# Narrow gate weights in a tile of their own, loaded behind five x tiles, with an x ring of five slots

## The chip, the core and the metric

The kernel runs on one core of a Trainium2 chip. The metric is the device time of one execution in microseconds. Before the change three timed runs took 2071.55, 2075.75 and 2076.64 us; their median, 2075.75, is the time that the change is measured against.

## The reference, cut to what matters

One decoder layer works on x of 1024 tokens by 2048 features. Its first step is an RMS norm and one wide projection; the last 16 of the 8208 columns are the narrow gates, b and a, of the delta-rule heads.

```
h = rms_norm(x, norm_w)
proj = einsum('btd,dc->btc', h, w_in)            # w_in: 2048 x 8208
q1, q2, k1, k2, v_da, gate_da = ...              # columns 0 to 4095, differential attention
qkv, z = ...                                     # columns 4096 to 8191, gated DeltaNet
b_raw = proj[..., 8192:8200]                     # narrow gates
a_raw = proj[..., 8200:8208]
...
return x + einsum('btc,cd->btd', mixed, w_out)   # then the final RMS norm
```

## The kernel before

The wide projection is done as two-level block products: the tokens are split into two halves and the features into two halves, and seven products of sums of blocks (the list ORDER) replace eight plain ones. The left operands are the weights, 256 columns per job, the right operands are seven combinations of the normalised and transposed x: B11, B21 and B22 are blocks, T1 to T4 differences of blocks. Each is kept in SBUF as a high and a low float16 part ("h" and "l", the tiles hb).

The start of the kernel makes these operands. Eight tiles of 128 tokens are taken in the order SEQ = 4, 0, 5, 1, 6, 2, 7, 3, that is in four pairs, one tile of each token half. For each tile, `scales` has ScalarE square both halves and sum them (jkw<-xt) and GpSimd take the power (rs); `scale` has VectorE multiply each half by rs and the norm weights (xt<-xt,rs,nwb). Then `combine` takes over: `turn` transposes four 128x128 blocks at a time on TensorE into PSUM banks (bka, bkb, side), `sums` and `make` subtract T1, T3, T2 and T4 on VectorE (the profile calls these tiles T), and `parts` splits everything into high and low parts, on ScalarE, VectorE or GpSimd. T1 to T4 have one buffer each. A tile of x is free once its last block is transposed ("turned").

The narrow weights, 2048 rows of 16 columns, are loaded once (abw). `narrow` squares and sums them on ScalarE, finds a scale over TensorE, VectorE and GpSimd, and writes the scaled high part on ScalarE and the low part on VectorE (abst). `narrow_sums` multiplies them with the finished token columns in four steps. Before the change abw lies in the buffer of T4 (line 791), so the first T4 waits for "abst" (lines 697 and 698).

The weights of the wide jobs are loaded as raw tiles (`weights`, `room`), two per job, three buffers. For each job ScalarE squares four blocks (jkw<-raw), TensorE, VectorE and GpSimd find the scales (f, sc), and seven products' weights are split into whi (ScalarE) and wlo (VectorE). The first two products of the first job, `early`, run column by column while the start goes on; all others (`products`) run at full width afterwards.

All loads of the start go through one SyncE queue. What is issued when, on it and on the engines, is decided when the program is built: `Planner` keeps one lane per task, books each instruction and each transfer with a cost (Op.cost, `transfer`), and always emits the instruction that could start first by this book. The engines then follow that order, each instruction waiting for its operands. `transfer` (lines 203 to 214) books pieces of up to 1024 bytes from w_in with 0.15 us each, sixteen at a time; a transfer's data count as there 2 us after its end (LAND).

Of the kernel before, what the change touches and what calls it, by code (L numbers as in the profile page):

```python
# [11 lines left out]
F32 = mybir.dt.float32  # L12
# [11 lines left out]
D = 2048  # L24
H = 8
P = 128
NT = T // P
ND = D // P
# [15 lines left out]
def bcast_rows(ap, n=P):  # L44
    return bass.AP(tensor=ap.tensor, offset=ap.offset, ap=[[0, n], *ap.ap])
# [220 lines left out]
class Planner:  # L266
# [104 lines left out]
    def dma(self, out, in_, bulk=False):  # L371
        self.pending.append(Copy(out, in_, bulk))
        self.nw[out.name] = self.nw.get(out.name, 0) + 1
        self.nr[in_.name] = self.nr.get(in_.name, 0) + 1
# [93 lines left out]
def hybrid_trunk(ctx: ExitStack, tc: tile.TileContext, a, out):  # L468
# [4 lines left out]
    dma = plan.dma  # L473
# [21 lines left out]
    w_v = w_in.rearrange("(a p) c -> p a c", p=P)  # L495
# [23 lines left out]
    done = set()  # L519
    box = {}  # L520

    def when(*keys):
        return lambda: all(k in done for k in keys)

    def junk(n):
        return cst.tile([P, D // 2], BF16, "jkw")[:, :n]
# [34 lines left out]
    def wide():  # L561
        return ps.tile([P, 512], F32, "prod", 2)
# [11 lines left out]
    def pow2_floor(dst, src):  # L574
        yield pool.tensor_tensor(out=dst, in0=src, in1=mhalf[:, :free_len(dst)], op=ALU.pow)
        yield dve.tensor_scalar(out=dst.bitcast(I32), in0=dst.bitcast(I32), scalar1=0x7F800000, scalar2=None,
                                op0=ALU.bitwise_and)
# [4 lines left out]
    SEQ = (4, 0, 5, 1, 6, 2, 7, 3)  # L582
    xt = {}

    def normalise(xs, abw):
        nwb = xs.tile([P, D], F32, "nwb")
        nw16 = xs.tile([P, ND], F32, "nw16")
        dma(nw16, a["norm_w"][0].rearrange("(p a) -> p a", p=P))
        half_d = [slice(k * (D // 2), (k + 1) * (D // 2)) for k in range(2)]

        def load(m):
            if m >= 4:
                yield when(("turned", m - 4))
            t = xt[SEQ[m]] = xs.tile([P, D], F32, "xt", 4)
            dma(t, x[SEQ[m] * P:(SEQ[m] + 1) * P, :])
            done.add(("loaded", m))

        def rest():
            for m in range(4, 8):
                yield from load(m)  # L600
        for m in range(2):
            yield from load(m)
        for sl in half_d:
            dma(nwb[:, sl], bcast_rows(a["norm_w"][0, sl]))
        dma(abw, w_v[:, :, 8192:8208])
        for m in range(2, 4):
            yield from load(m)
        done.add("loads")
        s_rest.push(rest())
        dma(gdn_w, a["gdn_norm_w"].rearrange("o p -> p o"))  # L610
        dma(sub_w, a["da_subln_w"].rearrange("o p -> p o"))
        nmx = xs.tile([P, 2], F32, "nmx")
        yield dve.tensor_reduce(out=nmx[:, 0:1], in_=nw16, axis=AX.X, op=ALU.max)
        yield dve.tensor_reduce(out=nmx[:, 1:2], in_=nw16, axis=AX.X, op=ALU.min, negate=True)
        yield dve.tensor_tensor(out=nmx[:, 0:1], in0=nmx[:, 0:1], in1=nmx[:, 1:2], op=ALU.max)
        pt = wide()
        yield pe.transpose(out=pt[:1, :P], in_=nmx[:, 0:1], identity=ident)
        big = xs.tile([1, 1], F32, "big")
        yield dve.tensor_reduce(out=big, in_=pt[:1, :P], axis=AX.X, op=ALU.max)
        yield dve.tensor_scalar(out=big, in0=big, scalar1=1e-18, scalar2=2.0 ** -7, op0=ALU.max, op1=ALU.mult)  # L620
        yield dve.tensor_tensor(out=big, in0=big, in1=big, op=ALU.mult)
        yield pe.matmul(pt[:, :1], ones[:1], big, start=True, stop=True)
        hsq = xs.tile([P, 1], F32, "hsq")
        yield dve.tensor_copy(hsq, pt[:, :1])
        hsc = xs.tile([P, 1], F32, "hsc")
        yield from pow2_floor(hsc, hsq)
        yield dve.reciprocal(hun, hsc)
        rs = {}

        def scales():  # L630
            for m, tb in enumerate(SEQ):
                yield when(("loaded", m))
                ss = xs.tile([P, 2], F32, "ss", 2)
                for k, sl in enumerate(half_d):
                    yield act.activation(junk(D // 2), xt[tb][:, sl], AF.Square, accum_out=ss[:, k:k + 1])
                ms = xs.tile([P, 1], F32, "ms", 2)
                yield dve.tensor_tensor(out=ms, in0=ss[:, 0:1], in1=ss[:, 1:2], op=ALU.add)
                yield dve.tensor_scalar(out=ms, in0=ms, scalar1=1.0 / D, scalar2=EPS, op0=ALU.mult, op1=ALU.add)
                if m >= 4:
                    yield when(("normed", SEQ[m - 4], 1))  # L640
                r = xs.tile([P, 1], F32, "rs", 4)
                yield pool.tensor_tensor(out=r, in0=ms, in1=mhalf[:, 0:1], op=ALU.pow)
                yield pool.tensor_tensor(out=r, in0=r, in1=hsc, op=ALU.mult)
                rs[tb] = r

        def scale():
            for i in range(4):
                pair = SEQ[2 * i:2 * i + 2]
                for k, sl in enumerate(half_d):
                    for tb in pair:  # L650
                        yield lambda: tb in rs
                        yield dve.scalar_tensor_tensor(out=xt[tb][:, sl], in0=xt[tb][:, sl], scalar=rs[tb],
                                                       in1=nwb[:, sl], op0=ALU.mult, op1=ALU.mult)
                        done.add(("normed", tb, k))

        s_scales.push(scales())
        s_scale.push(scale())

    def combine(xs):
        turns = [(n, nm) for n in range(8) for nm in ("B12", "B11", "B22", "B21")]  # L660
        turned, gone = [0], set()
# [32 lines left out]
        def make(n, m, l, r):  # L694
            if n:
                yield when(("split", m, n - 1))
            elif m == "T4":
                yield when("abst")
            t = sb[m, n] = xs.tile([P, 512], F32, m)
            yield dve.tensor_tensor(out=t, in0=l, in1=r, op=ALU.subtract)  # L700
            done.add((m, n))
# [51 lines left out]
    abu = small("abu", [P, 1])  # L753

    def narrow(xs, abw):
        yield when("loads")
        abst = xs.tile([P, ND, 32], F16, "abst")
        abq = xs.tile([P, 1], F32, "abq")
        f2 = xs.tile([P, 1], F32, "abf")
        abs_ = xs.tile([P, 1], F32, "abs")  # L760
        pt = box["ab"] = ps.tile([P, 512], F32, "av")
        yield act.activation(junk(256).rearrange("p (a c) -> p a c", a=ND), abw, AF.Square, accum_out=abq)
        yield pe.matmul(pt[:, :1], ones, abq, start=True, stop=True)
        yield dve.tensor_scalar(out=f2, in0=pt[:, :1], scalar1=2.0 ** -28, scalar2=1e-37, op0=ALU.mult, op1=ALU.max)
        yield from pow2_floor(abs_, f2)
        yield act.activation(abst[:, :, :16], abw, AF.Copy, scale=abs_)
        yield dve.scalar_tensor_tensor(out=abst[:, :, 16:], in0=abw, scalar=abs_, in1=abst[:, :, :16],
                                       op0=ALU.mult, op1=ALU.subtract)
        done.add("abst")
        yield dve.reciprocal(abu, abs_)  # L770
        s_nsum.push(narrow_sums(abst))

    def narrow_sums(abst):
        pt = box["ab"]
        for i in range(4):
            yield when(("cols", i))
            cs = slice(i * P, (i + 1) * P)
            for m, (n, g, r) in enumerate(NARROW):
                bh, bl = hb[n]
                c0 = (r * 4 + i) * 32  # L780
                for k in range(NH):
                    yield pe.matmul(pt[:, c0:c0 + 32], bh[:, k, cs], abst[:, g * NH + k], start=m < 3 and k == 0,
                                    stop=False, block=i)
                    yield pe.matmul(pt[:, c0:c0 + 16], bl[:, k, cs], abst[:, g * NH + k, :16], start=False,
                                    stop=m != 2 and k == NH - 1, block=i)
        done.add("narrow")

    def startup():
        with ExitStack() as st:
            xs = rpool(st, "xs")  # L790
            abw = xs.tile([P, 512], F32, "T4")[:, :256].rearrange("p (a c) -> p a c", a=ND)
            s_norm.push(normalise(xs, abw))
            s_narrow.push(narrow(xs, abw))
            yield from combine(xs)
            yield when("narrow", ("cols", 3))
        box["ev"] = rpool(right, "ev")
        lead.push(decay())
        lead.push(acc_loads())
# [917 lines left out]
    z_job(6)  # L1716

    outputs.push(startup())
    weights_.push(weights())
    main.push(products())  # L1720
# [207 lines left out]
```

## Time and profile before

| | us |
|---|---|
| profiled execution | 2082.34 |
| its span | 2080.6 |
| PE busy in the span | 1922.2 |
| VectorE busy | 1533.1 |
| ScalarE busy | 1058.7 |
| GpSimd busy | 362.2 |
| median of three timed runs | 2075.75 |

Times are taken from one profiled execution, counted from the start of its span. PE is TensorE, DVE is VectorE, ACT is ScalarE, POOL is GpSimd and SPq is the queue in which SyncE issues transfers. Nearly all instructions have line 369, because the planner emits them there; they are told apart by the tiles that they write and read.

### The profile page before, as it was taken

What the parts mean: (1) busy time and instruction counts of PE and PEld (TensorE: products, weight loads), DVE (VectorE), ACT (ScalarE), POOL (GpSimd) and SP (SyncE); (2) the same over time, 40 slices, a digit from 0 to 9 for tenths busy, and PEclk for the clock granted to TensorE, in tenths of its full rate; (3) what the DMA queues carried; (4) which work ended last, traced back from release to release, by engine and by line L of the source; (5) the groups of instructions that cost most, each with busy time, mean ns of one, the idle gap of its engine ahead of it and who ended that gap; (6) DMA issues with size and microseconds to landing.
All of it is one profiled execution on the core that took longest, in us unless ns stands there. A gap on an engine that the chain in (4) does not pass through costs nothing.

```text
span 2080.6 us, 28925 instructions
## 1 busy us (share of the span) xinstructions
PE 1922.2 (92%) x10221; PEld 1185.3 (57%) x10221; DVE 1533.1 (74%) x2831; ACT 1058.7 (51%) x2261; POOL 362.2 (17%) x383
## 2 busy tenths in 40 slices
PE   3699999999998899998999999899998999999896
PEld 3644455444443345454665555455555888888785
DVE  6776877877999973789887879788897566645343
ACT  6645555554344434476665657565675334434122
POOL 4503113220212201111212111111122110210000
PEclk7699999999999999998999999999999999999998
DMA  9046566456435686643557754555345676737322
GB/s 244 3 94 166 115 152 184 111 155 179 122 61 69 107 167 154 155 114 102 146 143 128 136 107 111 126 116 132 100 119 186 204 229 227 235 139 282 108 89 101
DMA packets 234498, 292.28 MB, mean 140 GB/s; under 512 B 51745, under 2 KB 160497, under 8 KB 231921
## 3 DMA queue, kind: packets, MB, share of 16 engines
q1 hardware_dynamic: 234352, 290.43, 54.6%
q8 instruction: 81, 1.33, 0.3%
q14 instruction: 65, 0.52, 0.1%
HBM read 206.44 MB, written 85.50 MB: 140 GB/s over the span
## 4 chain that ended last, share of the span: by engine, by line
PE 65%; DVE 14%; DMA 10%; issue 4%; ACT 4%; POOL 2%; SPq 1%; POOLq 0%; DVEq 0%; ACTq 0%
PE prod L369 43%; PE bka L369 6%; PE bkb L369 6%; PE av L369 5%; PE side L369 4%; DVE wlo L369 2%; DMA raw<-in_w_in_dram 2%; DVE c L369 2%; DVE raw L369 1%; SPq L401 1%; DVE A L369 1%; ACT jkw L369 1%; DVE tmp L369 1%; ACT whi L369 1%; DMA gq<-c 1%
## 5 line engine op out<-in xcount | busy, mean ns | idle before, releaser
L369 PEld LDWEIGHTS <-whi 128*128 128x128 f16 x3680 | 360.3, 100 | 410.2 <-issue 42.4
L369 PEld LDWEIGHTS <-wlo 128*128 128x128 f16 x1840 | 184.2, 100 | 210.9 <-DVE wlo L369 20.4
L369 ACT ACTIVATE whi<-raw,sc 128x1024 f16<-128x1024 f32 x160 | 182.6, 1146 | 207.7 <-PE prod L369 111.1
L369 DVE SCALAR_TENSOR_TENSOR wlo<-raw,sc,whi 128x1024 f16<-128x1024 f32 x160 | 206.1, 1293 | 20.9 <-ACT whi L369 20.6
L369 ACT ACTIVATE jkw<-raw 128x1024 bf16<-128x1024 f32 x140 | 147.2, 1051 | 50.7 <-DMA raw<-in_w_in_dram 30.6
L369 POOL TENSOR_TENSOR sum<-raw 128x1024 f32<-128x1024 f32 x32 | 79.1, 2473 | 293.9 <-DVE wlo L369 246.2
L369 PE MATMUL prod<-T2h,wlo 128*128 128x512 f16 (+1 forms) x280 | 103.2, 370 | 7.9 <-DVE wlo L369 7.9
L369 PE MATMUL prod<-B11h,whi 128*128 128x512 f16 (+1 forms) x280 | 103.7, 372 | 5.1 <-ACT whi L369 5.1
L369 PE MATMUL prod<-B11h,wlo 128*128 128x512 f16 (+1 forms) x280 | 103.3, 371 | 5.0 <-DVE wlo L369 5.0
L369 DVE SCALAR_TENSOR_TENSOR wlo<-sum,sc,whi 128x1024 f16<-128x1024 f32 x64 | 82.1, 1283 | 34.1 <-ACT whi L369 32.9
L369 PE MATMUL prod<-T4h,whi 128*128 128x512 f16 x256 | 99.1, 387 | 7.9 <-DVE U L369 7.9
L369 PE MATMUL prod<-T2h,whi 128*128 128x512 f16 (+1 forms) x280 | 103.0, 369 | 2.6 <-ACT whi L369 2.6
L369 PE MATMUL prod<-B11l,whi 128*128 128x512 f16 (+1 forms) x280 | 103.5, 372 | 0.0
L369 PE MATMUL prod<-T3h,whi 128*128 128x512 f16 x256 | 97.5, 381 | 6.2 <-ACT q L369 6.2
L369 PE MATMUL prod<-B21h,whi 128*128 128x512 f16 x256 | 99.0, 387 | 4.4 <-DVE V L369 4.4
L369 PE MATMUL prod<-T2l,whi 128*128 128x512 f16 (+1 forms) x280 | 103.1, 369 | 0.0
L369 PE MATMUL prod<-T4l,whi 128*128 128x512 f16 x256 | 99.1, 387 | 0.0
L369 PE MATMUL prod<-B21l,whi 128*128 128x512 f16 x256 | 99.0, 387 | 0.0
L369 PE MATMUL prod<-B21h,wlo 128*128 128x512 f16 x256 | 99.0, 387 | 0.0
L369 PE MATMUL prod<-T4h,wlo 128*128 128x512 f16 x256 | 98.9, 386 | 0.0
L369 PE MATMUL prod<-T3l,whi 128*128 128x512 f16 x256 | 97.6, 381 | 0.0
L369 PE MATMUL prod<-T1l,whi 128*128 128x512 f16 x256 | 97.4, 380 | 0.0
(644 smaller groups left out, 4912.3 us busy)
## 6 DMA issues: line engine op xcount, KB each, us to landing
raw<-in_w_in_dram SPq DMA_DIRECT2D x64, 1024.0 KB, 10.9
B11h<-in_w_out_dram SPq DMA_DIRECT2D x25, 1024.0 KB, 5.3
qst<-qd SPq DMA_DIRECT2D x256, 64.0 KB, 2.6
xt<-in_x_dram SPq DMA_DIRECT2D x8, 1024.0 KB, 7.4
qd<-c SPq DMA_DIRECT2D x32, 256.0 KB, 3.1
B11l<-in_w_out_dram SPq DMA_DIRECT2D x7, 1024.0 KB, 6.9
raw<-in_x_dram SPq DMA_DIRECT2D x6, 1024.0 KB, 8.0
out_dram<-raw SPq DMA_DIRECT2D x12, 512.0 KB, 3.6
```

The lines of the kernel that those rows point to most:

```text
L369: op.fn(*op.args, **op.kw)
L401: (self.nc.scalar if d.bulk else self.nc.sync).dma_start(out=d.out, in_=d.in_)
```

## The change

The ring of x tiles gets a fifth slot, so five x tiles can be loaded without waiting for one to be turned; the ring of their scales follows. The narrow weights get a tile of their own of 1 KB a partition and are loaded behind the fifth x tile in place of between the second and the third. `narrow` starts on that load's mark in place of the mark "loads". The first T4 waits for nothing of the narrow weights.

```diff
--- before.py
+++ after.py
@@ -589,23 +589,25 @@
         half_d = [slice(k * (D // 2), (k + 1) * (D // 2)) for k in range(2)]
 
         def load(m):
-            if m >= 4:
-                yield when(("turned", m - 4))
-            t = xt[SEQ[m]] = xs.tile([P, D], F32, "xt", 4)
+            if m >= 5:
+                yield when(("turned", m - 5))
+            t = xt[SEQ[m]] = xs.tile([P, D], F32, "xt", 5)
             dma(t, x[SEQ[m] * P:(SEQ[m] + 1) * P, :])
             done.add(("loaded", m))
 
         def rest():
-            for m in range(4, 8):
+            for m in range(5, 8):
                 yield from load(m)
         for m in range(2):
             yield from load(m)
         for sl in half_d:
             dma(nwb[:, sl], bcast_rows(a["norm_w"][0, sl]))
-        dma(abw, w_v[:, :, 8192:8208])
         for m in range(2, 4):
             yield from load(m)
         done.add("loads")
+        yield from load(4)
+        dma(abw, w_v[:, :, 8192:8208])
+        done.add("abw")
         s_rest.push(rest())
         dma(gdn_w, a["gdn_norm_w"].rearrange("o p -> p o"))
         dma(sub_w, a["da_subln_w"].rearrange("o p -> p o"))
@@ -636,9 +638,9 @@
                 ms = xs.tile([P, 1], F32, "ms", 2)
                 yield dve.tensor_tensor(out=ms, in0=ss[:, 0:1], in1=ss[:, 1:2], op=ALU.add)
                 yield dve.tensor_scalar(out=ms, in0=ms, scalar1=1.0 / D, scalar2=EPS, op0=ALU.mult, op1=ALU.add)
-                if m >= 4:
-                    yield when(("normed", SEQ[m - 4], 1))
-                r = xs.tile([P, 1], F32, "rs", 4)
+                if m >= 5:
+                    yield when(("normed", SEQ[m - 5], 1))
+                r = xs.tile([P, 1], F32, "rs", 5)
                 yield pool.tensor_tensor(out=r, in0=ms, in1=mhalf[:, 0:1], op=ALU.pow)
                 yield pool.tensor_tensor(out=r, in0=r, in1=hsc, op=ALU.mult)
                 rs[tb] = r
@@ -694,8 +696,6 @@
         def make(n, m, l, r):
             if n:
                 yield when(("split", m, n - 1))
-            elif m == "T4":
-                yield when("abst")
             t = sb[m, n] = xs.tile([P, 512], F32, m)
             yield dve.tensor_tensor(out=t, in0=l, in1=r, op=ALU.subtract)
             done.add((m, n))
@@ -753,7 +753,7 @@
     abu = small("abu", [P, 1])
 
     def narrow(xs, abw):
-        yield when("loads")
+        yield when("abw")
         abst = xs.tile([P, ND, 32], F16, "abst")
         abq = xs.tile([P, 1], F32, "abq")
         f2 = xs.tile([P, 1], F32, "abf")
@@ -788,7 +788,7 @@
     def startup():
         with ExitStack() as st:
             xs = rpool(st, "xs")
-            abw = xs.tile([P, 512], F32, "T4")[:, :256].rearrange("p (a c) -> p a c", a=ND)
+            abw = xs.tile([P, 256], F32, "abw").rearrange("p (a c) -> p a c", a=ND)
             s_norm.push(normalise(xs, abw))
             s_narrow.push(narrow(xs, abw))
             yield from combine(xs)
```

## Rows read from the trace of the kernel before

**Rows 1.** The page, part 1: busy us (share of the span) xinstructions of each engine.
```profile
PE 1922.2 (92%) x10221; PEld 1185.3 (57%) x10221; DVE 1533.1 (74%) x2831; ACT 1058.7 (51%) x2261; POOL 362.2 (17%) x383
```

**Rows 2.** Windows of the start: stretch, length, busy time of each engine, granted clock, DMA.
```profile
core 0: us, PE busy (x) PEld busy (x) DVE busy (x) ACT busy (x) POOL busy (x), PEclk, DMA share, GB/s
0.00:98.90 98.90, 49.19 (x549) 43.17 (x550) 70.90 (x115) 61.62 (x111) 50.90 (x60) 0.73 0.48 130
11.94:34.30 22.36, 9.53 (x82) 7.78 (x82) 16.55 (x28) 13.35 (x26) 12.16 (x13) 0.79 0.99 210
34.30:50.70 16.40, 8.17 (x48) 6.92 (x48) 14.95 (x20) 11.49 (x21) 9.62 (x9) 0.60 0.88 277
```

**Rows 3.** Chain of waits in order of time: start, length, what.
```profile
98.91 6.48 PE prod L369 x46
```

**Rows 4.** Timeline of DVE: start, length, instruction, out<-in, idle before it and releaser.
```profile
19.49 0.68 DVE L369 TENSOR_TENSOR T<-bkb,T 128x512 f32<-128x512 f32 x1
...
24.62 0.69 DVE L369 TENSOR_TENSOR T<-bka,T 128x512 f32<-128x512 f32 x1
...
47.43 0.68 DVE L369 TENSOR_TENSOR T<-bkb,T 128x512 f32<-128x512 f32 x1
...
53.98 1.30 DVE L369 TENSOR_SCALAR sc<-sc 128x2 int32<-128x2 int32 x2 [1.79 <-POOL sc L369]
...
65.95 2.48 DVE L369 SCALAR_TENSOR_TENSOR xt<-xt,rs,nwb 128x1024 f32<-128x1024 f32 x2
...
128.99 0.36 DVE L369 TENSOR_SCALAR sc<-sc 128x2 int32<-128x2 int32 x2 [1.71 <-POOL sc L369]
```

**Rows 5.** Timeline of ACT, columns as in the group before.
```profile
23.56 0.51 ACT L369 ACTIVATE abst<-T,abs 128x256 f16<-128x256 f32 x1 [1.78 <-DVE abs L369]
23.97 1.04 ACT L369 ACTIVATE jkw<-xt 128x1024 bf16<-128x1024 f32 x1
...
37.30 1.05 ACT L369 ACTIVATE jkw<-raw 128x1024 bf16<-128x1024 f32 x1
...
38.48 1.06 ACT L369 ACTIVATE jkw<-raw 128x1024 bf16<-128x1024 f32 x1
...
49.85 1.06 ACT L369 ACTIVATE jkw<-raw 128x1024 bf16<-128x1024 f32 x1
...
50.89 0.62 ACT L369 ACTIVATE T4h<-T 128x512 f16<-128x512 f32 x1
...
55.12 1.15 ACT L369 ACTIVATE whi<-raw,sc 128x1024 f16<-128x1024 f32 x1 [3.62 <-DVE sc L369]
```

**Rows 6.** Timeline of SPq, and DMA issues of short windows: xcount, KB, us to landing.
```profile
3.51 0.64 SPq L401 DMA_DIRECT2D T<-in_w_in_dram  x1
T<-in_w_in_dram SPq DMA_DIRECT2D x1, 128.0 KB, 10.5
...
4.19 8.21 SPq L401 DMA_DIRECT2D xt<-in_x_dram  x1
xt<-in_x_dram SPq DMA_DIRECT2D x2, 1024.0 KB, 7.4
...
14.14 0.44 SPq L401 DMA_DIRECT2D raw<-in_w_in_dram  x1
raw<-in_w_in_dram SPq DMA_DIRECT2D x1, 1024.0 KB, 14.6
...
raw<-in_w_in_dram SPq DMA_DIRECT2D x3, 1024.0 KB, 20.3
```

**Rows 7.** Window of the second pair's densest ten microseconds, columns as in group 2.
```profile
40.00:50.00 10.00, 4.51 (x21) 4.13 (x20) 9.37 (x15) 7.63 (x16) 7.19 (x7) 0.67 0.78 296
```

**Rows 8.** Timeline of POOL, columns as in group 4.
```profile
52.12 1.15 POOL L369 TENSOR_TENSOR T2l<-T,T2h 128x512 f16<-128x512 f32 x1
...
53.92 1.14 POOL L369 TENSOR_TENSOR T4l<-T,T4h 128x512 f16<-128x512 f32 x1
```

**Rows 9.** A late window, and PE's longest wait in it (total, times, longest).
```profile
1300.00:1350.00 50.00, 40.52 (x212) 23.59 (x211) 35.56 (x70) 26.79 (x62) 5.07 (x7) 0.90 0.58 123
...
PE bkb L369 <- DMA gv<-o: 7.1, 1, 7.1
```

## The prediction

> **What bounds the kernel now.** I read the page first, then the windows of the start, then the order of transfers, ScalarE and VectorE. The page has PE busy for 92% of the span [rows 1], so what is left to win is PE's idle time, 158.4 us. The windows show where an edit to the start can reach: up to 98.9 us PE is busy for only 49.2 us, and VectorE, with 70.9, is the fullest engine [rows 2]. From 98.91 us the chain is PE at products [rows 3]. So the start ends when the last token columns are split, and a microsecond saved there is a microsecond of the span, provided the later order stays.
>
> The start works on four pairs of token tiles (4,0), (5,1), (6,2), (7,3). The other two windows are cut where VectorE begins to scale the first pair (11.94), where it begins with the second (34.30), and where it ends the second's last split (50.70): in the first stretch of 22.36 us it works 16.55, in the second of 16.40 it works 14.95 [rows 2]. The third pair's second tile is scaled at 65.95 [rows 4]. Two things stand in the first stretch. T4 of the first pair is subtracted at 24.62 although T2 was begun at 19.49 [rows 4]: the narrow weights lie in T4's buffer until their scaled copies, the first of them ScalarE's at 23.56, are made [rows 5]. And ScalarE squares the third x tile only at 23.97, behind that copy [rows 5].
>
> No transfer holds these back. The narrow load is issued at 3.51 and lands 10.5 later, at 14.0; the fourth x tile, issued at about 12.4, lands 7.4 later, at 19.8 [rows 6]. The planner expected something else. It books the narrow load, 2048 pieces of 64 bytes, with 2048 x 0.15/16 = 19.2 us (lines 209 to 214), an x tile with 2.6 and a raw weight tile with 9.6, one behind the other, and adds 2 us. By this book the narrow weights are there at 30.6, the third and fourth x tile at 33.2 and 35.9, the raw tiles at 45.6, 55.2 and 64.8, the fifth and sixth x tile at 67.4 and 70. I use the book for nothing but the order of instructions, which is fixed when the program is built; durations are the trace's.
>
> **The change part by part.** *Order of loads.* Three x tiles pass the narrow load. In the book the third, fourth and fifth x tile are now there at 14.0, 16.7 and 19.3, the narrow weights at 38.5, the raw tiles at 48.2, 57.8 and 67.4, and the sixth x tile at 70 as before. On the chip the first two raw tiles, which now land at 28.7 (14.14 + 14.6) and 34.9 (about 14.6 + 20.3, the middle one of three) [rows 6], stand behind one more x tile and come 2.9 later: two x tiles came in the 5.8 us between the narrow load's landing and the fourth's. The SyncE queue issues in order: the small gdn_w and sub_w loads, the raw tiles and the last x tiles are queued behind the fifth tile and the narrow load. None of them is first used before ScalarE's square of raw at 37.30 [rows 5], where the first raw tile would be there at 31.6. The one wait that is new for a DMA, the sixth tile's on the first tile's last transpose, takes the place of the fifth tile's. All of this costs nothing while raw is used at 37 or later; without that cover it would cost the 2.9 us.
>
> *T4's own buffer.* The wait on the copies goes; T4 can follow T2 and its transposes at about 20.1 in place of 24.6. What is late next is VectorE itself, so this opens at most the 5.81 us that it stands idle in that stretch (22.36 - 16.55).
>
> *The second pair moves up.* With its squares due at 14 and 16.7 the planner puts the second pair's scaling, transposes and splits among those of the first. I bound the end of the second pair by VectorE's work. From 11.94 to 50.70 it is busy 16.55 + 14.95 = 31.5 us [rows 2]; the first half of the fifth tile comes into it too, 1.2 us (two such steps take 2.48 [rows 4]), together 32.7. With no idle time at all the end would be 11.94 + 32.7 = 44.6 in place of 50.70; with none of the idle time gone it stays 50.7. I take the share of the densest stretch of this work, 9.37 of 10 us [rows 7]: 32.7/0.937 = 34.9, end at 46.8.
>
> *The weights' squares lose their cover.* Now the first raw tile is squared at 37.30 and 38.48 and the second up to 49.85, in gaps of the second pair; ScalarE's last split of that pair follows at 50.89 [rows 5]. With the raw tiles due at 48.2 and 57.8 in the book and the second pair over before that, all four squares stand behind the pair: 4 x 1.18 (37.30 to 38.48 [rows 5]) = 4.7 us in series. They start when ScalarE has the last T4, which I put 1.4 us ahead of VectorE's end (T4 was subtracted at 47.43, 3.3 us before 50.70; the subtraction takes 0.69 and two splits 0.62 each [rows 4, 5]). Behind them runs the chain of the scales to the first whi: 4.2 us now (the last square ends at 50.9, 49.85 + 1.06, whi starts at 55.12 [rows 5]). Of it the GpSimd split at 52.12, which stands ahead of sc, takes 1.0, and two VectorE steps on sc that take 1.30 beside the split at 53.92, and 0.36 without one at 128.99 [rows 4, 8], take 0.9. Those splits are done by then, so 2.3. The first whi then starts at 46.8 - 1.4 + 4.7 + 2.3 = 52.4, against 55.12: 2.7 us earlier. From the ends it is 50.2 (4.9 earlier) and 56.3 (1.2 later).
>
> *From the first whi on.* The third pair's second tile was scaled 10.83 us behind the first whi (65.95 - 55.12 [rows 4, 5]), behind two whi and the squares of both tiles. The fifth tile's squares are now done before, but the sixth tile's due time in the book is what it was, 70, so its squares may fall behind a third whi and a raw square: 0 to 1.1 us later. I take 0.5. The fourth pair and the narrow sums of the last columns stay in order, so PE's stream begins some 2.2 us before 98.91. Extra SBUF (8 KB and 1 KB a partition) costs no instruction.
>
> **The sum.** 2.7 - 0.5 = 2.2 us off the start. The profiled execution took 2082.34 us, its span 2080.6; its sum becomes 2080.1. The median of the three timed runs is 2075.75, 6.6 lower; the same 2.2 off it gives 2073.5. The forecast's own range, 4.9 earlier to 1.2 later without the 0.5, is 2070.8 to 2077.
>
> One rule speaks against the overlap. The rows: the two steps on sc take 1.30 us beside a GpSimd split and 0.36 without [rows 4, 8], so a meeting costs 0.9. The Trainium skill, SBUF — State Buffer, section "SBUF: two separate sides", says that VectorE and GpSimd share one port pair as an exclusive lock, and that the loser waits for the whole instruction. The trace agrees (1.30 against 0.36, with the split's end at 55.06 between them). What it would make of the time is the second rival.
>
> **The rivals.** *First: the gain goes through whole.* If the planner finds a place for the raw squares among the second pair, as it does now, the first whi hangs on the second raw tile's landing alone: 34.9 + 2.9 = 37.8, two squares 2.4, the chain of 4.2: 44.4, 10.7 earlier; with pairs three and four as now that is 2065.0. For it: ScalarE is busy only 13.35 of 22.36 and 11.49 of 16.40 us in the two stretches [rows 2], and transfers allow it. Against it: VectorE's floor of 44.6 for the second pair, and the book's 57.8 for the raw tile. Half of it already passes the mark below, so its range is 2065 to 2069.5. Chance 0.21.
>
> *Second: the overlap is paid at the port.* The first pair's eight GpSimd splits (1.15 each [rows 8]) come to lie beside the second pair's four scaling steps and its casts. Should each of the eight stretch a VectorE step by 0.9, the second pair ends 7.2 later than summed, and the whole is 7.2 - 2.2 = 5.0 slower: 2080.8. For it: the meeting at 53.98. Against it: the planner orders around the port (function ported), and a step that reads PSUM, like T4's 0.69 at 24.62 [rows 4], is none that the planner counts for it. Chance 0.12.
>
> *Third, slower: the later order is dealt anew.* Every raw tile of the first two jobs is 2.6 us later in the book, so the planner's choices from there on may fall otherwise, on every engine. The place: a stretch far behind the start where PE runs dry, as it does from 1300 on, with 40.52 busy of 50 us and 7.1 in one wait for a DMA of gv [rows 9]. Its price is one such gap more, 9.5 us (50 - 40.52); it decides from the point where one operand more of a head is put behind a DMA that lands late. 9.5 - 2.2 is 7.3 slower, 2083. For it: such a gap exists, and nothing in the book, whose transfer times differ from the trace's as shown, guards against the next. Against: the same number can close. Chance 0.13.
>
> *Fourth: it does little.* The squares in series, the 1.1 us and scattered waits take the gain: 2075 to 2079, one place being the narrow chain itself, which ends in the copy at 23.56 [rows 5] and now falls into the second pair's end. Chance 0.10. The forecast keeps 0.44.
>
> **How the numbers follow.** Predicted is the likeliest, 2073.5. About 0.3%, 6.2 us, is what a measurement of this kernel can tell from no change; the marks are 2069.5 and 2082. Faster: the first rival with 0.21 and 0.02 of the forecast's fringe, 0.23. Slower: the third, 0.13, and 0.01 of the second, 0.14. Within: 0.63. For the range I leave out the third (0.13) and the lowest part of the first (about 0.05): 2065.5 to 2081.
>
> **What would show it.** Right: T4 of the first pair at about 20 and without idle time before it; the third tile's square at about 15; VectorE's end of the second pair at 45 to 48; the four raw squares in a row behind it; first whi at 50 to 54; PE's product stream from about 96.5. The first rival: raw squares among the second pair and the first whi below 47. The second: VectorE steps of over 1 us beside GpSimd splits before 45 us. The third: a start shortened by 2 us or more with a longer span, and windows behind 110 us in which PE is less busy than before. Wrong would be a raw tile or the sixth x tile named as what ScalarE waits for, or a second pair that still starts behind 30 us.

## The result

The changed kernel took 2092.80 us (median of 4 runs, 2090.63 to 2100.07) against 2073.65 us before (4 runs, 2070.82 to 2076.64). The ratio is 1.0101, 95% interval 1.0083 to 1.0120: slower by about 19 us, where 2073.5 was predicted with a range up to 2081.

The profiled execution of after took 2090.63 us, its span is 2088.9. Below is part 1 of its page, which answers [rows 1].

```profile
PE 1926.7 (92%) x10221; PEld 1189.6 (57%) x10221; DVE 1523.7 (73%) x2829; ACT 1057.5 (51%) x2261; POOL 379.3 (18%) x385
```

PE is idle for 2088.9 - 1926.7 = 162.2 us, 3.8 more than before, and busy for 4.5 us more with the same 10221 matmuls. VectorE runs two instructions fewer than before and GpSimd two more, although the change moves none: the planner has dealt some steps otherwise.

**The start did what the change says.** The windows of after, cut where the first pair's scaling begins, where the second's begins and where its last split ends, and the late window of [rows 9]; columns as in [rows 2]:

```profile
0.00:94.00 94.00, 49.76 (x549) 43.16 (x550) 70.71 (x115) 61.85 (x111) 54.14 (x60) 0.84 0.50 137
11.62:28.20 16.58, 7.87 (x32) 6.23 (x32) 15.53 (x26) 12.69 (x24) 10.00 (x12) 1.00 0.95 253
28.20:46.20 18.00, 9.28 (x59) 7.59 (x60) 17.60 (x26) 12.45 (x26) 16.78 (x13) 0.94 1.03 220
1300.00:1350.00 50.00, 40.78 (x218) 24.28 (x216) 36.86 (x74) 25.86 (x58) 5.35 (x7) 0.90 0.62 127
```

PE does in 94.0 us what took it 98.9 (549 matmuls in both). VectorE is idle for 1.05 us in the first pair's stretch (before 5.81) and 0.40 in the second's (before 1.45). The window from 1300, which the third rival had named, is as it was: 40.78 against 40.52.

The timeline of VectorE in after, which answers [rows 4]; columns as there:

```profile
19.95 0.69 DVE L369 TENSOR_TENSOR T<-bka,T 128x512 f32<-128x512 f32 x1
...
44.06 1.50 DVE L369 SCALAR_TENSOR_TENSOR abst<-abw,abs,abst 128x256 f16<-128x256 f32 x1
...
45.56 0.67 DVE L369 TENSOR_TENSOR B21l<-bkb,B21h 128x512 f16<-128x512 f32 x1
...
51.40 0.36 DVE L369 TENSOR_SCALAR sc<-sc 128x2 int32<-128x2 int32 x2 [0.82 <-POOL sc L369]
...
63.51 2.48 DVE L369 SCALAR_TENSOR_TENSOR xt<-xt,rs,nwb 128x1024 f32<-128x1024 f32 x2 [0.92 <-POOL rs L369]
```

ScalarE in after, which answers [rows 5], and PE's first stretch of products in the chain of waits, which answers [rows 3]:

```profile
14.64 1.06 ACT L369 ACTIVATE jkw<-xt 128x1024 bf16<-128x1024 f32 x1
...
44.81 1.08 ACT L369 ACTIVATE jkw<-raw 128x1024 bf16<-128x1024 f32 x1
...
46.02 1.06 ACT L369 ACTIVATE jkw<-raw 128x1024 bf16<-128x1024 f32 x1
...
47.20 1.06 ACT L369 ACTIVATE jkw<-raw 128x1024 bf16<-128x1024 f32 x1
...
48.38 1.06 ACT L369 ACTIVATE jkw<-raw 128x1024 bf16<-128x1024 f32 x1
...
51.60 1.15 ACT L369 ACTIVATE whi<-raw,sc 128x1024 f16<-128x1024 f32 x1 [2.07 <-DVE sc L369]
```

```profile
94.00 6.43 PE prod L369 x46
```

T4 of the first pair comes at 19.95, the third tile's square at 14.64, the four raw squares stand in a row, the first whi starts at 51.60 and PE's products at 94.00, 4.9 us earlier than before. The products of the two traces, counted in order, keep that distance (4.9 to 5.1) up to about 530 us. So by the medians 24 us are lost behind that point (19.15 + 4.9). The two profiled executions show 13.2 of them, since that of before took 8.7 us more than the median of its kernel, and that of after 2.2 less. None of it lies at an instruction that the change touches.

**Where the two orders part.** `Planner` books every product with one of two costs, by a model of TensorE's clock (class `Clock`, line 235). Which one is decided anew at the steps of a fixed grid of book time that begins at 0. The changed start is 2.6529 us shorter in the book, and behind it all instructions of both books stand in one order, 2.65 us apart, up to 520 us of the changed book. That shift is no whole number of the grid's steps. At 520 the book of before has its products at half rate, 0.4327 apart, that of after at full rate, 0.2163 apart, and from there on "which instruction could start first" has other answers, on every engine. The first to differ on PE: the changed kernel does six more products ahead of a weights' sum (side<-ssq,ones). The kernel's own book ends at 2052.0 for before and at 2071.3 for after.

### The profile page after: what moved, and what is told of

Read it like the earlier page. It is cut to its first block, busy times and chain, and to the rows that moved or that the text cites. A ratio compares the mean times of both kernels' runs of the same rounds, so it can differ in the third digit from the quotient of the medians.

```text
span 2088.9 us, 28936 instructions
## 1 busy us (share of the span) xinstructions
PE 1926.7 (92%) x10221; PEld 1189.6 (57%) x10221; DVE 1523.7 (73%) x2829; ACT 1057.5 (51%) x2261; POOL 379.3 (18%) x385
## 4 chain that ended last, share of the span: by engine, by line
PE 69%; DVE 11%; DMA 11%; ACT 5%; issue 3%; SPq 1%; POOL 1%; POOLq 0%; ACTq 0%; DVEq 0%
PE prod L369 47%; PE bka L369 6%; PE bkb L369 6%; PE av L369 5%; PE side L369 5%; DVE raw L369 2%; DVE wlo L369 2%; SPq L401 1%; ACT jkw L369 1%; DMA B11h<-in_w_out_dram 1%; DVE c L369 1%; DMA t<-td 1%; ACT whi L369 1%; DMA gq<-c 1%; DVE tmp L369 1%
## 5 line engine op out<-in xcount | busy, mean ns | idle before, releaser
L369 PE MATMUL prod<-T3h,wlo 128*128 128x512 f16 x256 | 97.9, 383 | 0.0
L369 PE MATMUL prod<-T1h,wlo 128*128 128x512 f16 x256 | 97.7, 381 | 0.0
```

Of the source, the lines that this page charges most:

```text
L369: op.fn(*op.args, **op.kw)
```

## The experiments

Two theories stood against each other. **A**: the loss is the order behind the start, dealt anew by the grid. **B**: the loss comes from the change itself, its later raw tiles, its fuller buffers or its other queue order.

### The same start with the old order, the old start with the new order

The edit moves the grid from the end of the start on. In after_grid it stands in the changed kernel with -2.6529, which gives every engine the order of before behind 101 us of the book; in before_dealt it stands in the kernel before with +2.6529, which gives the order of after.

```diff
-        self.window, self.work, self.half = 0, 0.0, True
+        self.window, self.work, self.half, self.late = 0, 0.0, True, 0.0
...
-        while t >= (self.window + 1) * WINDOW:
+        while t >= (self.window + 1) * WINDOW + self.late:
...
-            edge = (self.window + 1) * WINDOW
+            edge = (self.window + 1) * WINDOW + self.late
...
             yield when("narrow", ("cols", 3))
+        plan.clock.late = -2.6529
```

> The changed kernel, and when its start is over the window grid of the planner's clock is moved by -2.6529 us. By that the planner decides as in the kernel before, and behind the start every engine has the instruction order of before; the start is that of the changed kernel. Theory A (the loss is the later order, dealt anew at about 530 us because the planner's clock windows lie on a fixed grid): the 4.9 us of the start stay, 2073.65 - 4.9 = 2068.7 us. Theory B (the loss comes from the change itself: the larger tiles, their places in SBUF, the transfers): it stays at about 2092 us.

> The kernel before, with nothing of the change; only the window grid of the planner's clock is moved by +2.6529 us when the start is over, which gives every engine behind the start the instruction order of the changed kernel. Theory A: it pays the loss without the change, the changed kernel's 2092.8 plus the 4.9 us that its start had won, 2097.7 us. Theory B: 2073.65 us as before.

Measured: after_grid 2068.69 us (12 runs) against 2072.66 for before beside it (29 runs), ratio 0.9974 (0.9964 to 0.9984). before_dealt 2101.72 us (4 runs), ratio 1.0132 (1.0116 to 1.0147). Both are A's, and before_dealt, with none of the change's edits in it, loses as after does. It took 4.0 us more than A had said, so the order costs 29.1 us behind the start of before and 24.1 behind that of after; why the two differ by 5 was not found. The later raw tiles of the third rival are out as well: after_grid has them just as late, in the book and on the chip.

The gain of after_grid is 4.0 us, 0.9 less than A had said. One stretch of 64 products shows where a part of the start's gain goes again; before, then after_grid, from the chain of waits:

```profile
140.29 13.92 PE prod L369 x64
...
134.47 15.61 PE prod L369 x64
```

It begins 5.8 us earlier and ends 4.1 earlier. The granted clock is 0.57 between 134 and 138 us in after_grid, and 1.00 between 138 and 144 in before. The order is the same; only the start ahead of it differs.

The two orders can be compared behind one and the same start. The windows of after_grid in the two stretches where after lags most:

```profile
650.00:700.00 50.00, 38.05 (x176) 18.01 (x176) 46.80 (x62) 26.21 (x53) 8.73 (x5) 0.91 0.56 74
1600.00:1650.00 50.00, 49.08 (x287) 42.42 (x286) 25.17 (x76) 17.51 (x52) 7.37 (x6) 0.98 0.68 211
```

and of after:

```profile
650.00:700.00 50.00, 32.43 (x145) 15.59 (x146) 46.18 (x55) 24.08 (x50) 5.29 (x3) 0.83 0.43 55
1600.00:1650.00 50.00, 41.49 (x227) 34.17 (x228) 23.09 (x60) 16.69 (x48) 2.82 (x6) 0.90 0.71 239
```

In the first, PE gets 31 matmuls less done, in the second 60. Its waits between 650 and 700 (line waited for, total, times, longest) are these in after_grid:

```profile
PE side L369 <- DVE un L369: 6.3, 2, 5.5
PE prod L369 <- DVE U L369: 2.3, 1, 2.3
PE prod L369 <- ACT q L369: 1.6, 1, 1.6
PE prod L369 <- DVE V L369: 1.6, 1, 1.6
PE side L369 <- DVE c L369: 0.3, 1, 0.3
```

these in after:

```profile
PE side L369 <- DVE c L369: 11.0, 2, 9.1
PE prod L369 <- ACT q L369: 5.1, 1, 5.1
PE prod L369 <- DVE wlo L369: 1.6, 2, 0.9
```

and these in before_dealt, between 655 and 700:

```profile
PE side L369 <- DVE c L369: 11.1, 2, 9.1
PE prod L369 <- ACT q L369: 4.9, 1, 4.9
PE prod L369 <- DVE wlo L369: 1.6, 2, 0.9
```

The old start with the new order has the waits of after to a tenth or two: the rows go with the order. In PE's queue the transposes of c come next, and they wait for VectorE, which works 9.6 to 10 us of ten there, with the A updates among its steps. What follows is in windows of 10 us of after:

```profile
660.00:670.00 10.00, 5.14 (x26) 2.45 (x24) 10.00 (x11) 5.32 (x10) 0.00 (x0) 0.93 0.37 32
670.00:680.00 10.00, 1.12 (x4) 0.85 (x5) 9.63 (x12) 2.66 (x7) 0.00 (x0) 0.50 0.93 125
680.00:690.00 10.00, 9.55 (x35) 4.39 (x35) 9.34 (x12) 4.18 (x9) 0.00 (x0) 0.72 0.08 28
```

PE works 1.12 of 10 us, its granted clock is at 0.50, the lower of the two levels (1.2 GHz), and in the next ten us, though PE is busy for 9.55, it stands at 0.72 and PE does 35 matmuls; in after_grid it does 46 from 700 to 710, at 0.95. Here a wait is paid twice, as idle time and in the clock behind it. The start of after_grid, to set beside that of after above:

```profile
0.00:94.00 94.00, 47.40 (x551) 41.06 (x552) 69.56 (x115) 61.84 (x111) 54.43 (x60) 0.78 0.50 137
```

Behind 94 us after has 15.1 us more idle time on PE than after_grid and is busy for 3.9 us longer with the same matmuls (1926.7 - 49.76 against 1920.4 - 47.40), together the 19.0 us between the spans. One pair of executions is little for the 3.9: over the whole span PE is busy for 1917.5 to 1922.5 us in the six traces with the order of before, and for 1926.7 and 1931.2 in the two with that of after. With PE's products counted in order, those of after are 19.6 us late at 772 (by the time of after_grid), 0.7 early at 995, since other work was done in between, 10.6 late at 1216, still 10.5 at 1587, and 20.0 at 1824; from 1825 on both kernels have one order again. So the waits between 650 and 700 show what the new order does, but what the span keeps is lost between 1000 and 1216 and between 1587 and 1824. The longest wait of after in the first of these stretches is for a load that after_grid waits for too; after_grid, then after:

```profile
PE bkb L369 <- DMA kst<-kdl: 1.7, 1, 1.7
...
PE bka L369 <- DMA kst<-kdl: 4.2, 1, 4.2
```

In the second, between 1600 and 1650, after has one wait of 2.8 us for ScalarE's T2h that after_grid has not.

### A book without the grid

In both kernels the planner books every product behind the start at full rate, so nothing there hangs on the grid. Both then have one order behind the start, a third one. before_flat is the kernel before with this edit, after_flat the changed kernel.

```diff
     def run(self, t0, cost):
+        if self.flat:
+            return t0 + cost
...
             yield when("narrow", ("cols", 3))
+        plan.clock.flat = True
```

> [...] The order of the start is untouched; the order behind it is a third one, neither that of before nor that of after. Its book ends at 2049.8. A (the loss is the order): the book's end has followed the chip to some us in three orders so far, so about 2072, between 2065 and 2085. B (the loss comes from the changed start itself): nothing is said of this run alone, it is the base for the next.

> The changed kernel, with the same edit. Behind the start it has the same instructions in the same order as the run before this one, on every engine; its book ends at 2047.1. A: the time is that of the run before this less what the start gives, 4.9 us (3 to 7), about 2067. B: the changed start or the larger ring costs later whatever the order is, and it is some 19 us slower than the run before this, about 2091.

Measured: before_flat 2092.21 us (4 runs), after_flat 2088.29 us (6 runs), beside 2074.41 for before (17 runs); ratios 1.0089 (1.0076 to 1.0103) and 1.0071 (1.0058 to 1.0084). At equal order the change is 3.9 us faster, as A says. The size forecast for before_flat, 2072, fell: this order costs 18 us, though its book ends 2.2 earlier than that of before. With the clock left out, the book's end was 20 us off.

### Two more orders

The grid moved by -2.5 in the changed kernel (after_best) and by -1.6 in the kernel before (before_m16); otherwise the edit is that of after_grid.

> The changed kernel with the windows of the book moved by -2.5 us behind the start, in place of -2.6529: another order behind the start, whose book ends at 2045.8, 3.5 ahead of that with -2.6529 (chip 2068.7). A, and the book's end tells the chip's to some us: 2065, between 2061 and 2070. If the book only tells large differences, it is anywhere in 2061 to 2078. B: 2092, as after.

> The kernel before, unchanged in loads, buffers and waits, with the windows of the book moved by -1.6 us behind the start. Its book ends at 2083.7 in place of 2052.0. A: 2105, between 2095 and 2112, with a start that is that of before. B: 2073.7, as before.

Measured: after_best 2077.39 us (12 runs), ratio 1.0018 (1.0009 to 1.0026); before_m16 2106.40 us (4 runs), ratio 1.0155 (1.0141 to 1.0170). The second is a hit within 1.4 us, and shows the kernel before losing 32 us by its order alone. The first is a miss: the book put it 3.5 us ahead of after_grid, the chip 8.7 behind, nearly all of it behind 1130 us, with products counted in order (1.4 ahead there, 8.7 behind at 1219). With the clock in it, the book's end told differences of 20 us here, not of 3.

### The parts of the change, with the order of before behind them

Each has the grid moved by what its own start is shorter in the book, so all have the order of before behind the start. own_grid has only the tile of its own and no wait before T4, with the loads and the ring of before. order_grid has only the order of loads and the ring of five; the narrow weights stay in T4's buffer, and T4 waits. late4_grid has the whole change but for the fifth slot: the narrow load stands behind the fourth tile.

```diff
-            abw = xs.tile([P, 512], F32, "T4")[:, :256].rearrange("p (a c) -> p a c", a=ND)
+            abw = xs.tile([P, 256], F32, "abw").rearrange("p (a c) -> p a c", a=ND)
...
-            elif m == "T4":
-                yield when("abst")
```

> One part alone: the narrow weights have their own tile and the first T4 waits for nothing of them, while the loads stand in the order of before and the x ring has four slots. The clock's grid is moved by -2.541 us behind the start, so that the later order is that of before. My step for T4 says that it could start at about 20 in place of 24.6; with VectorE late next I expect 4 us off the start, 2069.7 us. If the loads' order carries the gain, it is 2073.65 us.

> The other part alone: five x tiles ahead of the narrow load and a ring of five slots, but the narrow weights still in T4's buffer, so the first T4 waits for their scaled copies. Grid moved by -2.6301 us behind the start, later order that of before. If the order of loads carries the gain: the second pair fills VectorE while T4 waits, 3 to 5 us off, 2069 to 2071 us. If T4's own buffer carries it: 2073.65 us or slower.

> The change without its fifth slot: narrow weights in a tile of their own and loaded behind four x tiles, x ring of four as before, T4's wait gone; windows of the book moved by -2.541 us behind the start, so that the order behind it is that of before. P (the fifth slot carries part of the start's gain, since only with it the fifth tile is squared ahead of the raw weights): the sixth tile and with it PE's stream come about 2.5 us later than with it, 2071.5. Q (passing the third and fourth x tile ahead of the narrow load is enough): a start 4 to 6 us shorter than before, 2068, between 2066 and 2070.

| kernel | T4, first pair | first whi | xt x2 of the third pair | PE's stretch of 31 products | median, us | ratio (interval) |
|---|---|---|---|---|---|---|
| before | 24.62 | 55.12 | 65.95 | 118.95 | 2072.7 | 1 |
| own_grid | 19.80 | 55.84 | 70.21 | 121.02 | 2076.70 | 1.0017 (1.0007 to 1.0027) |
| order_grid | 32.78 | 54.46 | 65.19 | 116.08 | 2070.41 | 0.9993 (0.9982 to 1.0005) |
| late4_grid | 20.28 | 52.94 | 67.32 | 118.36 | 2076.01 | 1.0018 (1.0004 to 1.0032) |
| after_grid | 19.86 | 51.51 | 63.41 | 113.13 | 2068.69 | 0.9974 (0.9964 to 0.9984) |

Of the expectations, own_grid's 2069.7 failed, and so did its other value, 2073.65: it came out at 2076.70. order_grid's 2069 to 2071 held, though its interval includes no change. late4_grid missed both of its values, 2071.5 and 2068.

The start is read from the column of 31 products. Taking T4's wait away alone makes it 2.1 us longer, where a gain was expected. ScalarE in own_grid shows why:

```profile
26.59 0.41 ACT L369 ACTIVATE jkw<-abw 128x256 bf16<-128x256 f32 x1
...
29.39 0.51 ACT L369 ACTIVATE abst<-abw,abs 128x256 f16<-128x256 f32 x1 [2.30 <-DVE abs L369]
29.81 1.04 ACT L369 ACTIVATE jkw<-xt 128x1024 bf16<-128x1024 f32 x1
...
62.95 1.04 ACT L369 ACTIVATE jkw<-raw 128x1024 bf16<-128x1024 f32 x1
64.11 1.06 ACT L369 ACTIVATE jkw<-xt 128x1024 bf16<-128x1024 f32 x1
```

The narrow chain has lost its hurry, is put at 26.59, and the third tile's square, which the book still has behind it, comes at 29.81 in place of 23.97 [rows 5]. The fifth tile's squares fall behind the third whi and a raw square, to 64.11, where before has them at 56.18. The order of loads alone gives 2.9 us although T4 is 8 us later than before. T4's own buffer on top of it gives another 2.9 (113.13 against 116.08). So the x tiles that pass the narrow load carry half of the 5.8 us, and T4's buffer, which loses time by itself, gives the other half once they pass; of that half 0.6 is one stretch of 46 products, which took 5.72 us in after_grid and 6.27 in order_grid. In the medians order_grid and after_grid lie only 1.7 us apart. late4_grid has the early squares, but its fifth tile is squared only from 61.22 on, behind the third whi and a raw square, so its third pair comes late and 0.6 us are left: without the fifth slot most of the gain is gone.

The medians of own_grid and order_grid follow their starts within 2 us. That of late4_grid does not: its start is 0.6 shorter than before's, its median 3.2 longer, its runs lie between 2067.87 and 2081.57, and its profiled execution is the fastest of them. The kernels that ran beside it scatter as widely, before from 2067.12 to 2079.89 and the repeat of after_grid from 2062.75 to 2077.78. What moves them was not found.

### after_grid once more

> The changed kernel with the order of before behind the start, a second time, beside the run before this one. A: 4.9 us under the kernel before, 2068.7. If the first time was chance: 2073 or more.

Measured: 2069.29 us (12 runs) against 2072.81 (23 runs), ratio 0.9976 (0.9961 to 0.9992). The changed kernel with the order of before is the fastest of all that ran.

## Why the prediction was wrong

The medians in one table (before is given from the run of the change; beside the experiments it took 2072.66, 2074.41 and 2072.81):

| order behind the start | start of before | start of after |
|---|---|---|
| that of before | 2073.65 | 2068.69, 2069.29 |
| that of after | 2101.72 | 2092.80 |
| book without the grid | 2092.21 | 2088.29 |
| grid moved by -1.6 | 2106.40 | not run |
| grid moved by -2.5 | not run | 2077.39 |

Each column spans more than 23 us, each row less than 9.

**The step that failed** is "so a microsecond saved there is a microsecond of the span, provided the later order stays". The proviso was given 0.13 to fail, with the argument that one gap may open and another close. What the runs show in its place: with the later order kept, 4.9 us off the start are 4.0 off the time (after_grid); with the order that the change deals, the same start costs 24.1 more. The order was likely to change: the book's start changes its length by 2.65 us, the grid does not move, and every choice behind depends on both; after_best, whose grid is 0.15 us off, already has another order. That the order changes could have been read from the two built programs. Which way the time goes could not. But of the five orders that ran, that of before is the fastest: behind the same start the others cost 8.7 (grid at -2.5), 18.6 to 19.6 (no grid), 24.1 to 28.1 (that of after) and 32.8 us (grid at -1.6). So a new deal looks more likely to lose than to win, though four orders are few, and of two of them (the grids at -1.6 and -2.5) the book's end was known when they were tried.

**The third rival had the sign and the kind, a later order dealt anew, but not the trigger and not the size.** It named raw tiles due later in the book, and a price of one gap, 9.5 us, at a place like 1300 us. after_grid has the same raw tiles and loses nothing, and the window at 1300 is unchanged. Its reading of the book was off as well: only three raw tiles are later there, not all four of the first two jobs, and on the chip the fourth is issued 4.9 us earlier (99.97 against 104.88). The cause is the grid, and the price is 24 us between 514 and 1825 us, in waits and in the clock behind them.

**The start**, step by step. T4 at about 20: 19.95. No transfer holds it back: none is named as a releaser between 20 and 94 us. The raw tiles were to come 2.9 us later; the first was issued at 19.91 and landed some 15.5 later, at about 35.4, which is 6.7 later than before; it cost nothing, since raw is first squared at 44.81. The second pair's VectorE end at 46.8: 46.2. The four raw squares in a row behind it, 4.7 us: 44.81 to 49.44. The chain of 2.3 to the first whi: 2.2 (51.60 - 49.44), with sc at 0.36. First whi at 52.4: 51.60. The third pair 0.5 us late, bounds 0 to 1.1: its scaling began 10.83 us behind the first whi before [rows 4, 5] and 11.91 now, so 1.1.

**The term that was mis-sized most**: "The fourth pair and the narrow sums of the last columns stay in order", costed at no change. The whole start gave 4.9 us where 2.2 was summed. Of the 2.7 missing, 0.8 is the first whi, less 0.6 for the third pair's scaling. The third pair gets its last split 3.2 us earlier than before (75.86 against 79.09), 0.8 more than its scaling: of that, 0.52 is a wait of VectorE for B11h, which before has at 71.17 and after has not. The last 1.7 are the fourth pair's. In the trace of before VectorE waits there 1.19 for rs, 0.65 for bka, 0.47 for bkb and 0.43 for b; in after none of these waits is left. The last three, 1.55 together, are the gain. The first is none: from 76.47 on the three scaling steps of after run in one piece, but in 5.73 us, where those of before need 5.82 with the wait among them.

```profile
79.70 1.27 DVE L369 SCALAR_TENSOR_TENSOR xt<-xt,rs,nwb 128x1024 f32<-128x1024 f32 x1
82.17 3.35 DVE L369 SCALAR_TENSOR_TENSOR xt<-xt,rs,nwb 128x1024 f32<-128x1024 f32 x2 [1.19 <-POOL rs L369]
...
76.47 5.73 DVE L369 SCALAR_TENSOR_TENSOR xt<-xt,rs,nwb 128x1024 f32<-128x1024 f32 x3
```

The first two lines are of before, the third of after.

**The port** cost little before the first whi, as the forecast had it. The copy abst took 1.50 us beside a GpSimd split (44.13 to 45.28), where own_grid, without one beside it, has

```profile
29.93 0.48 DVE L369 SCALAR_TENSOR_TENSOR abst<-abw,abs,abst 128x256 f16<-128x256 f32 x1 [0.57 <-ACT abst L369]
```

That is 1.0 us more. Up to the second pair's end two more steps of VectorE are stretched: ms<-ss, 0.15 us elsewhere, took 0.52 at 24.28 and 1.11 at 29.39. Together it is 2.3 us, not eight times 0.9, and before lost 1.1 in the same two steps (0.74 at 30.23, 0.69 at 33.49). Behind it the fourth pair's three scaling steps took 5.73 us, where two alone take 2.48 [rows 4], beside four GpSimd steps: some 2 us more. The rule of the Trainium skill, SBUF — State Buffer, section "SBUF: two separate sides", by which a VectorE step with two inputs in SBUF, as this one, and a GpSimd step hold a shared port pair in turn, each for its whole instruction, agrees with the two rows of abst, 1.50 us beside a split and 0.48 without.

## What to carry to other kernels

Where a program orders its own instructions by a book in absolute time, an edit at its start is two edits: the one meant, and a new deal of all that follows. Before judging the first, print both orders and look for the first instruction that differs; then replay the old order behind the edit, or give both versions the same new one, and only that difference is the edit's. Here the edit was worth 4 us and the deal cost 24. A wait that is taken away may also move work ahead of what mattered, as with T4's, whose removal alone made the start longer.

## What the runs showed that was not expected

A stall of PE cost more than its length: with two waits of 9.1 and 5.1 us between 665 and 680 the granted clock was 0.50 in the ten us from 670 and 0.72 in the ten after, and behind 94 us a fifth of the loss (3.9 of 19.0) lies in matmuls that took longer, not in idle time. A start that ends earlier did not keep its whole lead even at the same order: 1.7 of 5.8 us went in one drop of the clock at 134 us. And executions of one and the same program scatter by up to 15 us (after_grid the second time: 2062.75 to 2077.78), so that differences of 3 us need a dozen runs of each.
